# A hybrid decoder layer on one core: adaLN steps behind tile statistics, threshold passes and rotation spread anew, bias rows loaded ahead, low parts of down weights behind the sum of M7, one store from ScalarE

## Chip, cores and metric

One core of a Trainium2 chip runs the whole layer. The metric is the device time in microseconds (us) of one execution, as the median of the runs. Engines: PE is TensorE (PEld is its weight load), DVE is VectorE, ACT is ScalarE, POOL is GpSimd, and SP is the queue that issues DMAs.

## What is computed

One decoder layer on a sequence of 1024 tokens of width 1024, all in float32:

```python
mod = jnp.dot(jax.nn.silu(c), w_ada) + b_ada
shift1, scale1, gate1, shift2, scale2, gate2 = [m[:, None, :] for m in jnp.split(mod, 6, axis=-1)]
h = _rmsnorm(x, norm1_w) * (1.0 + scale1) + shift1
(qa, ka, va, iq, ik, iw, qr, kr, vr, gr, ga, gb) = jnp.split(jnp.dot(h, w_in), ...)
...  # partial rotation of qa, ka, iq, ik over 16 of 64 channels
att = _dsa_attention(qa, ka, va, iq, ik, iw, topk)      # the 256 best keys of each row
y_a = jnp.dot(att, w_attn_proj)
ret = _retention(rotate(qr), rotate(kr) * 128 ** -0.5, vr)   # 4 heads, chunks of 128 tokens
y_r = jnp.dot(jax.nn.silu(gr) * _head_groupnorm(ret, gn_w), w_ret_proj)
merged = jax.nn.sigmoid(ga) * y_a + jax.nn.sigmoid(gb) * y_r
x = x + gate1 * jnp.dot(merged, w_out)
h2 = _rmsnorm(x, norm2_w) * (1.0 + scale2) + shift2
ffn = jnp.dot(jax.nn.silu(jnp.dot(h2, w_ffn_gate)) * jnp.dot(h2, w_ffn_up), w_ffn_down)
out = _rmsnorm(x + gate2 * ffn, final_norm_w)
```

## The kernel before

Nearly every product of two matrices is made of three: each factor is split into a high part, rounded on ACT, and a low part, the difference to it, taken on DVE or POOL; PE multiplies high by high, high by low and low by high. The large projections (the flow of `w_in` after retention, the FFN, the down projection) use a Strassen scheme with seven products, M1 to M7, for a block of two by two.

The order in which each engine works is fixed when the kernel is built. A planner walks through the program and places every instruction on its engine's queue by priority and by estimated times. `turns_after(a, b)` adds an order to that: `a` stands behind `b` on their engine's queue, without a semaphore. An engine works through its queue in order, so an instruction that must wait holds all that stand behind it.

The stages that the change touches, in order of time:

- **Scores and adaLN, from about 130 us.** PE projects V (L121 to L124) and makes index scores (L424, L425); DVE sums the scores (L432). Between them runs `mod_work`, a generator with one step for each of the chunks m = 2, 5, 3, 4 of the adaLN matrix and each k of 8: load 512 KB (`mw`, L515) and add it, scaled, to `macc` on DVE (L525, L527, 1024 columns a step). After the eight steps of m = 2 and m = 5 follows `mod_gate`: for each half it loads a bias row (`gateb`, one buffer, L558), sums `macc` over partitions with a product with `ones` (L561) into a bank of the `lg` tag (three buffers, which the scores use too), adds both on DVE (L562) and stores the result (L563). After m = 3 and m = 4 follows `mod_cols` (transposes and L548 to L552). Every step stands behind the last entry of `summed`, which holds the sums of scores. Sixteen calls fall into the V projection, two into each tile of the loop over `t` with `hp == 0` below, and what is left follows at its end.
- **The threshold passes.** DVE seeks the 256th largest score of each row by 32 counting passes over all scores (L463, six instructions a pass, then L468 and L483), and then makes the mask. `passes[n]` is the first instruction of pass n; some passes are told to stand behind other work by `turns_after`.
- **Retention, two head pairs `hp`.** The projection of q and k is rotated on POOL (L654 to L660). In the loop over nine `t`, `inner(t, e)` makes PE's product of q and k and multiplies it with the decay mask on DVE (L676), `chunk(t - 1, e)` multiplies it with v on PE, carries the state on DVE (L693, L695) and takes the statistics of the tile on DVE (`bn_stats` L701 and `bn_aggr` L702, the last one kept in `chunked[0]`). In the loop's tiles t = 2, 4, 6, 8, `passes[7]` to `passes[10]` (first pair) and `passes[18]` to `passes[21]` (second pair) are put behind that statistic.
- **The flow of 13 streams**, from about 500 us: each stream is 7 products of 12 matmuls (L841, L843, L845). Factors are prepared three products ahead: a sum on DVE (L799, L809), the high part on ACT (L755), the low part on POOL (L756; on DVE near both ends). `add` is the sum of a product into its quarter on DVE (L824). `behind(i)` runs after product i and puts one pass behind the newest sum every seven products. For partial rotation, `rope_load` fetches the 16 channels of q and k and the tables, and `rope_store` does four products on POOL (L991, L992, L994, L995), a difference and a sum on DVE (L993, L996), splits both results (ACT L755, POOL L756) and issues eight stores (L1002).
- **FFN and down projection, to the end.** `Stream.product` is used again. PE adds M4 onto the bank into which M7 was summed, so the first matmul of M4 waits until DVE has read the bank for `add("22")` of M7. `down_slot` makes the factors of the down products: a load, the high part on ACT (L1641), the low part on DVE or POOL (L1642). `final_norm` ends a tile: ACT scales the right half (L1691), DVE the left half (L1693), SP stores both (L1692, L1694).

Of the kernel before, what the change touches and what calls it, by code (L numbers as in the profile page):

```python
# [43 lines left out]
def tile_hybrid_layer(ctx: ExitStack, tc: tile.TileContext, x, c, w_ada, b_ada, norm1_w, w_in,  # L44
# [20 lines left out]
    def f32(ap):  # L65
        return ap.bitcast(F32)
# [433 lines left out]

    st_m = ctx.enter_context(ExitStack())
    modp = pool("modp", side="right", stack=st_m)
    ones = modp.tile([P, P], F32, name="ones")
    nc.vector.memset(ones, 1.0)

    def mod_work():

        steps = [(m, k) for m in (2, 5, 3, 4) for k in range(KT)]
        mw = {}

        def load(n):
            if n < len(steps):
                m, k = steps[n]
                mw[n] = modp.tile([P, D], F32, name="mw", bufs=2)
                ins = nc.sync.dma_start(out=mw[n], in_=w_ada[k * P:(k + 1) * P, m * D:(m + 1) * D])  # L515
                turns_after(ins, loaded[0])

        load(0)
        for n, (m, k) in enumerate(steps):
            load(n + 1)  # L520
            sc = silu_c[:, k:k + 1]
            behind = summed[-1] if summed else None
            if k == 0:
                acc = modp.tile([P, D], F32, name="macc", bufs=1)
                ins = nc.vector.tensor_scalar(acc, mw[n], sc, None, op0=ALU.mult)  # L525
            else:
                ins = nc.vector.scalar_tensor_tensor(acc, mw[n], sc, acc, op0=ALU.mult, op1=ALU.add)  # L527
            if behind is not None:
                turns_after(ins, behind)
            yield  # L530
            if k == KT - 1:
                if m in (2, 5):
                    mod_gate(m, m // 5, acc)
                else:
                    mod_cols(m, m - 3, acc)
                yield
# [14 lines left out]
        if i == 1:  # L551
            nc.vector.scalar_tensor_tensor(d, d, 1.0, colT[:, 64:72], op0=ALU.add, op1=ALU.mult)  # L552

    def mod_gate(m, i, acc):
        for hf in range(2):
            cs = slice(hf * H, (hf + 1) * H)
            g = modp.tile([P, H], F32, name="gateb", bufs=1)
            nc.sync.dma_start(out=g, in_=b_ada[m * D + hf * H:m * D + (hf + 1) * H]  # L558
                              .rearrange("(o d) -> o d", o=1).partition_broadcast(P))
            gp = ps_lg()  # L560
            nc.tensor.matmul(gp, lhsT=ones, rhs=acc[:, cs], start=True, stop=True)  # L561
            nc.vector.tensor_add(g, g, gp)  # L562
            nc.sync.dma_start(out=gate_d[i][:, cs], in_=g)  # L563
# [74 lines left out]
    for hp in range(2):  # L638
# [71 lines left out]
        for t in range(NT + 1):  # L710
# [11 lines left out]
            if t and t % 2 == 0:  # L722
                turns_after(passes[(6, 17)[hp] + t // 2], chunked[0])
            if hp == 0:
                for _ in range(2):
                    next(mgen, None)
            elif t == 2:
# [30 lines left out]
    class Stream:  # L758
# [4 lines left out]

        def __init__(self, env, w, c0):
            self.env, self.w, self.c0 = env, w, c0
            self.c, self.ready, self.blocks = {}, {}, {}
            self.early = ()
            self.next = self.t1 = None

# [51 lines left out]
            self.copied = nc.scalar.activation(self.c[c], ps, AF.Copy)  # L821

        def add(self, c, ps):
            self.env.added = nc.vector.tensor_add(self.c[c], self.c[c], ps)  # L824

        def product(self, m, after=None):

# [157 lines left out]
            nc.sync.dma_start(out=tab[a], in_=rope_c[:, a, cs])  # L985
        return r, tab

    def rope_store(hf, r, tab):
        cs = slice(hf * H, (hf + 1) * H)
        t = [f32(x) for x in ring_pair()]  # L990
        nc.gpsimd.tensor_mul(t[0], r[0], tab[0])  # L991
        nc.gpsimd.tensor_mul(t[1], r[1], tab[1])  # L992
        nc.vector.tensor_sub(t[0], t[0], t[1])  # L993
        nc.gpsimd.tensor_mul(r[0], r[0], tab[1])  # L994
        nc.gpsimd.tensor_mul(r[1], r[1], tab[0])  # L995
        nc.vector.tensor_add(r[1], r[1], r[0])  # L996
        for a, src in enumerate((t[0], r[1])):
            parts = ring_pair()
            split_block(src, *parts)
            for w, dst in enumerate((q_d, k_d)):  # L1000
                for i, part in enumerate(parts):
                    nc.sync.dma_start(out=dst[:, 8 * a:8 * a + 8, i, cs], in_=f32(part[64 * w:64 * w + 64]))  # L1002
# [21 lines left out]
    n_mid = len(seq)  # L1024
    seq += [(st, m) for st in flow[-2:] for m in ("M1", "M2")]
    seq += [(st, m) for m in ("M5", "M6", "M7", "M4", "M3") for st in flow[-2:]]
    rope, staged = {}, {}

    def behind(i):
        n, m = 2 + (i - 14) // 7, seq[i][1]  # L1030
        if i in (11, n_mid - 4):
            genv.lo_engine = None if i == 11 else nc.vector
        if i >= 15 and (i - 15) % 7 == 0 and 24 + (i - 15) // 7 < len(passes) - 1:
            turns_after(passes[24 + (i - 15) // 7], genv.added)
        if 14 <= i < n_mid:
            if m == "M1":
                flow[n + 1].open()
                flow[n].next = flow[n + 1]
            if n == 8 and m in ("M1", "M7"):
                rope[len(rope)] = rope_load(len(rope))  # L1040
            if n == 9 and m in ("M5", "M2"):
                rope_store(int(m == "M2"), *rope[int(m == "M2")])
        if i == n_mid:
            flow[-1].open()
        k = i - n_mid - 4
# [586 lines left out]
    def down_slot(src, lo_eng, scale=None, here=False):  # L1632
# [6 lines left out]
        if scale is not None:  # L1639
            nc.gpsimd.tensor_mul(raw, raw, scale)  # L1640
        nc.scalar.activation(slot[:, 0], raw, AF.Copy)  # L1641
        lo_eng.tensor_sub(slot[:, 1], raw, f32(slot[:, 0]))  # L1642
        return slot[:, 0], slot[:, 1]

    def down_factors(m, p):
# [37 lines left out]
    def final_norm(t, n_parts):  # L1683
# [5 lines left out]
        rs = const.tile([P, 16], F32, name="rs3", bufs=4)[:, 0:1]  # L1689
        nc.gpsimd.tensor_tensor(rs, last, half_pow[:, :1], op=ALU.pow)  # L1690
        nc.scalar.activation(xo[1], xo[1], AF.Copy, scale=rs)  # L1691
        nc.sync.dma_start(out=out[t * P:(t + 1) * P, H:], in_=xo[1])  # L1692
        nc.vector.scalar_tensor_tensor(xo[0], x1[t][:, :H], rs, fnorm[0], op0=ALU.mult, op1=ALU.mult)  # L1693
        nc.sync.dma_start(out=out[t * P:(t + 1) * P, :H], in_=xo[0])  # L1694

# [103 lines left out]
```

## Time and profile before

| | |
|---|---|
| median of 3 runs | 1747.34 us (1744.49 to 1750.73) |
| the profiled execution's own time | 1744.53 us |
| its span, first to last instruction | 1742.7 us |
| PE busy | 1685.4 us, 97% of the span |
| DVE busy | 1234.4 us, 71% |
| POOL busy | 856.8 us, 49% |
| ACT busy | 755.3 us, 43% |
| mean granted clock of PE | 0.995 of full speed |

The busy share of PE says how much of the span it had a matmul in hand; matmuls overlap, so the start of one to the start of the next is the better measure of pace. The idle time in front of a PE instruction, and what ended it, says what the rest of the kernel costs PE.

### The profile page before, as it was taken

What the parts mean: (1) busy time and instruction counts of PE and PEld (TensorE: products, weight loads), DVE (VectorE), ACT (ScalarE), POOL (GpSimd) and SP (SyncE); (2) the same over time, 40 slices, a digit from 0 to 9 for tenths busy, and PEclk for the clock granted to TensorE, in tenths of its full rate; (3) what the DMA queues carried; (4) which work ended last, traced back from release to release, by engine and by line L of the source; (5) the groups of instructions that cost most, each with busy time, mean ns of one, the idle gap of its engine ahead of it and who ended that gap; (6) DMA issues with size and microseconds to landing.
All of it is one profiled execution on the core that took longest, in us unless ns stands there. A gap on an engine that the chain in (4) does not pass through costs nothing.

```text
span 1742.7 us, 24594 instructions
## 1 busy us (share of the span) xinstructions
PE 1685.4 (97%) x8266; PEld 1391.7 (80%) x8266; DVE 1234.4 (71%) x2118; ACT 755.3 (43%) x1469; POOL 856.8 (49%) x855
## 2 busy tenths in 40 slices
PE   5899999999999999999999999999999999999998
PEld 4797777888887887888777888888888888878887
DVE  7528798898899577666576666885666555778664
ACT  3625542332454344530477235643333333445444
POOL 4563274583615578130346550055455554657573
PEclk9999999999999999999999999999999999999999
DMA  9535515412434356865761740044445444586652
GB/s 293 151 95 176 152 55 173 143 34 60 117 98 127 108 151 200 252 205 165 186 142 53 274 169 1 25 133 148 157 134 180 173 146 144 187 305 205 197 169 97
DMA packets 180063, 260.72 MB, mean 150 GB/s; under 512 B 13584, under 2 KB 111328, under 8 KB 177632
## 3 DMA queue, kind: packets, MB, share of 16 engines
q1 hardware_dynamic: 179936, 259.14, 47.6%
q8 instruction: 65, 1.06, 0.3%
q14 instruction: 62, 0.51, 0.1%
HBM read 192.51 MB, written 66.58 MB: 149 GB/s over the span
## 4 chain that ended last, share of the span: by engine, by line
PE 64%; DVE 3%; issue 1%; DMA 1%; POOL 1%; ACT 1%; SPq 0%; POOLq 0%; DVEq 0%; ACTq 0%
PE ya L843 4%; PE ya L841 4%; PE ya L845 4%; PE yb L843 3%; PE yb L841 3%; PE yb L845 3%; PE ya L1664 2%; PE ya L1663 2%; PE ya L1662 2%; PE pva L1183 2%; PE mm L841 2%; PE mm L843 2%; PE mm L845 2%; PE tra L1162 2%; PE lg L841 1%; PE lg L843 1%
## 5 line engine op out<-in xcount | busy, mean ns | idle before, releaser
L80 POOL TENSOR_TENSOR wlo<-wraw,whi 128x512 fp32r<-128x512 f32 (+2 forms) x116 | 147.9, 1285 | 136.6 <-ACT whi L77 100.1
L463 DVE TENSOR_SCALAR_CACHE_REDUCE eq<-score,cand 128x384 uint8<-128x384 f32 (+2 forms) x192 | 180.7, 941 | 4.0
L756 POOL TENSOR_TENSOR flo<-tmp,fhi 128x512 fp32r<-128x512 f32 x79 | 108.2, 1369 | 140.1 <-ACT fhi L755 100.5
L121 PE MATMUL mm<-whi,hT_hi 128*128 128x512 f32 (+1 forms) x432 | 162.0, 380 | 4.0 <-ACT qk L647 1.8
L123 PE MATMUL mm<-wlo,hT_hi 128*128 128x512 f32 (+1 forms) x432 | 161.6, 377 | 0.0
L124 PE MATMUL mm<-whi,hT_lo 128*128 128x512 f32 (+1 forms) x432 | 161.5, 376 | 0.0
L841 PE MATMUL ya<-hc,fhi 128*128 128x512 f32 x344 | 133.9, 390 | 2.0 <-DVE c L824 2.0
L843 PE MATMUL ya<-hc,fhi 128*128 128x512 f32 x344 | 134.1, 390 | 0.6 <-DVE hc L1302 0.6
L845 PE MATMUL ya<-hc,flo 128*128 128x512 f32 x344 | 133.1, 390 | 0.0
L1641 ACT ACTIVATE dslot<-draw 128x512 fp32r<-128x512 f32 x143 | 84.9, 627 | 93.1 <-DMA draw<-act_d 23.2
L756 POOL TENSOR_TENSOR flo<-raws,fhi 128x512 fp32r<-128x512 f32 x60 | 86.3, 1445 | 73.8 <-ACT fhi L755 42.4
L1642 DVE TENSOR_TENSOR dslot<-draw,dslot 128x512 fp32r<-128x512 f32 x81 | 86.4, 1098 | 50.7 <-ACT dslot L1641 49.3
L1642 POOL TENSOR_TENSOR dslot<-draw,dslot 128x512 fp32r<-128x512 f32 x62 | 95.5, 1554 | 53.0 <-ACT dslot L1641 51.0
L77 ACT ACTIVATE whi<-wraw 128x512 fp32r<-128x512 f32 (+2 forms) x116 | 67.2, 591 | 117.3 <-DMA wraw<-in_w_in_dram 56.6
L755 ACT ACTIVATE fhi<-tmp 128x512 fp32r<-128x512 f32 x82 | 51.5, 629 | 111.5 <-PE ya L843 57.2
L843 PE MATMUL yb<-hc,fhi 128*128 128x512 f32 x256 | 99.7, 390 | 0.0
L841 PE MATMUL yb<-hc,fhi 128*128 128x512 f32 x256 | 99.7, 389 | 0.0
L845 PE MATMUL yb<-hc,flo 128*128 128x512 f32 x256 | 99.5, 389 | 0.0
L121 PEld LDWEIGHTS mm<-whi,hT_hi 128*128 128x128 f32 x432 | 81.5, 190 | 16.1 <-ACT qk L647 2.2
L809 DVE TENSOR_TENSOR tmp<-raws 128x512 f32<-128x512 f32 x40 | 30.6, 768 | 86.7 <-POOL flo L756 86.7
L124 PEld LDWEIGHTS mm<-whi,hT_lo 128*128 128x128 f32 x432 | 81.7, 189 | 12.4
L1151 POOL TENSOR_SCALAR sx<-sx,mx 128x128 f32<-128x128 f32 (+7 forms) x64 | 47.4, 747 | 88.9 <-DVE mx L1150 66.3
(419 smaller groups left out, 4959.6 us busy)
## 6 DMA issues: line engine op xcount, KB each, us to landing
draw<-act_d SPq DMA_DIRECT2D x70, 256.0 KB
mw<-in_w_ada_dram SPq DMA_DIRECT2D x32, 512.0 KB
act_d<-c SPq DMA_DIRECT2D x58, 256.0 KB
raw<-in_w_in_dram SPq DMA_DIRECT2D x26, 512.0 KB
raws<-in_w_ffn_gate_dram SPq DMA_DIRECT2D x24, 512.0 KB
raws<-in_w_ffn_up_dram SPq DMA_DIRECT2D x24, 512.0 KB
dw<-in_w_ffn_down_dram SPq DMA_DIRECT2D x22, 512.0 KB
dw_d<-dw SPq DMA_DIRECT2D x10, 1024.0 KB
```

Of the source, the lines that this page charges most:

```text
L77: ins = nc.scalar.activation(hi[:, :n], raw[:, :n], AF.Copy)
L80: nc.gpsimd.tensor_sub(lo[:, :n], raw[:, :n], f32(hi[:, :n]))
L121: ins = nc.tensor.matmul(ps, lhsT=ahi, rhs=whi[:, :n], start=(i == 0), stop=False)
L123: nc.tensor.matmul(ps, lhsT=ahi, rhs=wlo[:, :n], start=False, stop=False)
L124: nc.tensor.matmul(ps, lhsT=alo, rhs=whi[:, :n], start=False, stop=(i == last))
L463: ins = [nc.vector.tensor_scalar(eq[:, :sc.shape[1]], sc, thr[j], None, op0=op, op1=ALU.add, accum_out=cnt[:, j:j + 1]) for j, sc in enume ...
L756: return ins, (eng or nc.gpsimd).tensor_sub(lo, src, f32(hi))
L841: mm = nc.tensor.matmul(ps, lhsT=whi[:, k, :], rhs=hhi[:, k, :], start=own and k == 0, stop=False, skip_group_check=True)
L843: nc.tensor.matmul(ps, lhsT=whi[:, k, :], rhs=hlo[:, k, :], start=False, stop=False, skip_group_check=True)
L845: nc.tensor.matmul(ps, lhsT=wlo[:, k, :], rhs=hhi[:, k, :], start=False, stop=k == 3, skip_group_check=True)
L1641: nc.scalar.activation(slot[:, 0], raw, AF.Copy)
L1642: lo_eng.tensor_sub(slot[:, 1], raw, f32(slot[:, 0]))
```

## The change

- In the loop over tiles of the first head pair, `summed` gets the statistic of the tile before (`chunked[0]`) from t = 1 on, so the adaLN steps issued there stand behind it on DVE.
- The bias row of a gate is loaded whole (512 KB with its copies on 128 partitions) after step k = 3 of its chunk, into one tile of 1024 columns, and both halves are taken from it. `ones` moves into the tile `spare`, which is free at that time.
- In the flow, the passes that stand behind the newest sum every seven products are 22 to 32 instead of 24 to 32.
- `rope_store` becomes the generator `rope_turn` in three turns: the four POOL products; the two DVE instructions; the splits and stores. It is called once a product, M1, M5, M6 for the first half and M3, M7, M2 for the second, where all of it was done at M5 and at M2 before. The second half's loads move from M7 to M6 of the stream before.
- `down_slot` puts the low parts of its calls 2 to 11 that are on DVE (five of them) behind `add("22")` of the last stream.
- The right half of the last tile is stored from ScalarE's queue.

```diff
-    ones = modp.tile([P, P], F32, name="ones")
+    ones = spare[:, :P]
     nc.vector.memset(ones, 1.0)
...
             if behind is not None:
                 turns_after(ins, behind)
+            if k == 3 and m in (2, 5):
+                bias = gate_bias(m)
             yield
             if k == KT - 1:
                 if m in (2, 5):
-                    mod_gate(m, m // 5, acc)
+                    mod_gate(m // 5, acc, bias)
...
+    def gate_bias(m):
+        bias = modp.tile([P, D], F32, name="gateb", bufs=1)
+        nc.sync.dma_start(out=bias, in_=b_ada[m * D:(m + 1) * D].rearrange("(o d) -> o d", o=1).partition_broadcast(P))
+        return bias
+
+    def mod_gate(i, acc, bias):
         for hf in range(2):
             cs = slice(hf * H, (hf + 1) * H)
-            g = modp.tile([P, H], F32, name="gateb", bufs=1)
-            nc.sync.dma_start(out=g, in_=b_ada[m * D + hf * H:m * D + (hf + 1) * H]
-                              .rearrange("(o d) -> o d", o=1).partition_broadcast(P))
+            g = bias[:, cs]
             gp = ps_lg()
             nc.tensor.matmul(gp, lhsT=ones, rhs=acc[:, cs], start=True, stop=True)
             nc.vector.tensor_add(g, g, gp)
...
             if hp == 0:
+                if t:
+                    summed.append(chunked[0])
                 for _ in range(2):
                     next(mgen, None)
...
-            self.env.added = nc.vector.tensor_add(self.c[c], self.c[c], ps)
+            self.env.added = self.added[c] = nc.vector.tensor_add(self.c[c], self.c[c], ps)
...
-    def rope_store(hf, r, tab):
+    def rope_turn(hf, r, tab):
+
         cs = slice(hf * H, (hf + 1) * H)
         t = [f32(x) for x in ring_pair()]
         nc.gpsimd.tensor_mul(t[0], r[0], tab[0])
         nc.gpsimd.tensor_mul(t[1], r[1], tab[1])
-        nc.vector.tensor_sub(t[0], t[0], t[1])
         nc.gpsimd.tensor_mul(r[0], r[0], tab[1])
         nc.gpsimd.tensor_mul(r[1], r[1], tab[0])
+        yield
+        nc.vector.tensor_sub(t[0], t[0], t[1])
         nc.vector.tensor_add(r[1], r[1], r[0])
+        yield
         for a, src in enumerate((t[0], r[1])):
...
-        if i >= 15 and (i - 15) % 7 == 0 and 24 + (i - 15) // 7 < len(passes) - 1:
-            turns_after(passes[24 + (i - 15) // 7], genv.added)
+        if i >= 15 and (i - 15) % 7 == 0 and 22 + (i - 15) // 7 < len(passes) - 1:
+            turns_after(passes[22 + (i - 15) // 7], genv.added)
...
-            if n == 8 and m in ("M1", "M7"):
-                rope[len(rope)] = rope_load(len(rope))
-            if n == 9 and m in ("M5", "M2"):
-                rope_store(int(m == "M2"), *rope[int(m == "M2")])
+            if n == 8 and m in ("M1", "M6"):
+                rope.append(rope_turn(len(rope), *rope_load(len(rope))))
+            if n == 9 and m != "M4":
+                next(rope[int(m in ("M3", "M7", "M2"))], None)
...
-        lo_eng.tensor_sub(slot[:, 1], raw, f32(slot[:, 0]))
+        ins = lo_eng.tensor_sub(slot[:, 1], raw, f32(slot[:, 0]))
+        if 2 <= n < 12 and lo_eng is nc.vector:
+
+            turns_after(ins, flow[-1].added["22"])
...
-        nc.sync.dma_start(out=out[t * P:(t + 1) * P, H:], in_=xo[1])
+        (nc.scalar if n_parts > 1 else nc.sync).dma_start(out=out[t * P:(t + 1) * P, H:], in_=xo[1])
```

## Rows read from the trace of the kernel before

**Rows 1.** The page: the span, PE, and the group of the counting passes

```profile
span 1742.7 us, 24594 instructions
...
PE 1685.4 (97%) x8266; PEld 1391.7 (80%) x8266; DVE 1234.4 (71%) x2118; ACT 755.3 (43%) x1469; POOL 856.8 (49%) x855
...
L463 DVE TENSOR_SCALAR_CACHE_REDUCE eq<-score,cand 128x384 uint8<-128x384 f32 (+2 forms) x192 | 180.7, 941 | 4.0
```

**Rows 2.** Waits of PE: who waited for whom, total us, times, longest us

```profile
PE tr L674 <- DVE inn L676: 4.7, 2, 3.4
...
PE lg L841 <- ACT whi L755: 2.1, 1, 2.1
...
PE mm L841 <- DVE kept L824: 2.0, 1, 2.0
...
PE lg L841 <- ACT kept L821: 1.4, 1, 1.4
```

**Rows 3.** Timeline, 182 to 187 us: start us, us, instruction, [idle before <- releaser]

```profile
182.00 0.33 SPq L558 DMA_DIRECT2D gateb<-in_b_ada_dram  x1
...
185.27 0.69 DVE L562 TENSOR_TENSOR gateb<-gateb,lg 128x512 f32<-128x512 f32 x1 [3.40 <-DMA gateb<-in_b_ada_dram]
...
186.01 0.39 PE L424 MATMUL lg<-khi,qst 128*128 128x256 f32 x1 [1.82 <-DVE gateb L562]
```

**Rows 4.** Timeline, 289 to 291 us, DVE and PE

```profile
289.31 1.28 DVE L527 SCALAR_TENSOR_TENSOR macc<-mw,colT,macc 128x1024 f32<-128x1024 f32 x1 [0.52 <-DMA mw<-in_w_ada_dram]
290.51 0.28 DVE L676 TENSOR_TENSOR inn<-tr,rmask 128x128 f32<-128x128 f32 x1
...
290.85 0.80 PE L674 MATMUL tr<-qkT 128*128 128x128 f32 x2 [3.38 <-DVE inn L676]
```

**Rows 5.** Windows: us, each engine's busy time (instructions), granted clock, DMA share, GB/s

```profile
290.85:294.30 3.45, 3.45 (x10) 2.85 (x10) 3.19 (x4) 0.38 (x1) 0.00 (x0) 0.53 0.58 172
310.00:320.00 10.00, 10.00 (x50) 8.52 (x49) 6.30 (x20) 3.46 (x7) 3.01 (x9) 1.00 0.08 26
340.00:350.00 10.00, 9.97 (x45) 7.97 (x44) 9.52 (x22) 4.39 (x11) 9.05 (x13) 1.00 0.79 251
680.00:690.00 10.00, 10.00 (x45) 8.23 (x44) 6.88 (x9) 2.50 (x4) 10.00 (x8) 1.00 0.66 193
720.00:730.00 10.00, 10.00 (x52) 8.26 (x51) 5.27 (x9) 5.48 (x10) 0.00 (x0) 1.00 0.90 284
```

**Rows 6.** Timeline at 413 us: PE at the first tile of the second pair

```profile
413.51 0.71 PE L674 MATMUL tr<-qkT 128*128 128x128 f32 x4 [1.31 <-DVE inn L676]
```

**Rows 7.** Timeline, 535 to 537 us, DVE and PE

```profile
535.27 0.61 DVE L463 TENSOR_SCALAR_CACHE_REDUCE eq<-score,cand 128x384 uint8<-128x384 f32 x1
...
536.54 0.50 PE L841 MATMUL mm<-hT_hi,whi 128*128 128x512 f32 x1 [2.01 <-DVE kept L824]
```

**Rows 8.** Timeline, 668 to 675 us, around the first rotation

```profile
668.00 1.74 POOL L995 TENSOR_TENSOR wlo<-wlo,whi 128x512 f32<-128x512 f32 x1
...
673.61 0.63 ACT L755 ACTIVATE whi<-whi 128x512 fp32r<-128x512 f32 x1 [2.78 <-DVE whi L993]
674.32 1.29 POOL L756 TENSOR_TENSOR wlo<-whi 128x512 fp32r<-128x512 f32 x1 [4.57 <-ACT whi L755]
```

**Rows 9.** Timeline, 1525 to 1530 us, DVE and PE

```profile
1525.01 1.77 DVE L1642 TENSOR_TENSOR dslot<-draw,dslot 128x512 fp32r<-128x512 f32 x1
...
1527.31 0.68 DVE L1642 TENSOR_TENSOR dslot<-draw,dslot 128x512 fp32r<-128x512 f32 x1
...
1528.52 0.68 DVE L824 TENSOR_TENSOR c<-c,ya 128x512 f32<-128x512 f32 x1
...
1529.25 0.50 PE L841 MATMUL ya<-hc,fhi 128*128 128x512 f32 x1 [1.68 <-DVE c L824]
```

**Rows 10.** Timeline at the end: the two last stores

```profile
1738.54 0.33 SPq L1692 DMA_DIRECT2D out_dram<-xo  x1
1739.28 0.33 SPq L1694 DMA_DIRECT2D out_dram<-xo  x1
```

More of the change, by code (lines that the diff above doesn't have):

```diff
@@ L552, in mod_cols @@
             nc.vector.scalar_tensor_tensor(d, d, 1.0, colT[:, 64:72], op0=ALU.add, op1=ALU.mult)
-    def mod_gate(m, i, acc):
+    def gate_bias(m):
[3 more added lines that the diff above has]
+    def mod_gate(i, acc, bias):
         for hf in range(2):
             cs = slice(hf * H, (hf + 1) * H)
-            g = modp.tile([P, H], F32, name="gateb", bufs=1)
-            nc.sync.dma_start(out=g, in_=b_ada[m * D + hf * H:m * D + (hf + 1) * H]
-                              .rearrange("(o d) -> o d", o=1).partition_broadcast(P))
+            g = bias[:, cs]
             gp = ps_lg()
@@ L765, in __init__ @@
             self.env, self.w, self.c0 = env, w, c0
-            self.c, self.ready, self.blocks = {}, {}, {}
+            self.c, self.ready, self.blocks, self.added = {}, {}, {}, {}
             self.early = ()
@@ L1026, in tile_hybrid_layer @@
     seq += [(st, m) for m in ("M5", "M6", "M7", "M4", "M3") for st in flow[-2:]]
-    rope, staged = {}, {}
+    rope, staged = [], {}
     def behind(i):
```

## Prediction

> **What bounds the kernel now.** The page comes first: PE is busy 1685.4 of 1742.7 us, 97% [rows 1]. No other engine comes near it, so the kernel can only gain where PE stands idle or runs at the low clock, 57 us in all, part of it at the start, which the change doesn't touch. The second view is the list of what PE waited for, the third the timeline around each of those waits. After the start only a few waits exceed 1 us, and the parts of the change lie beside five of these places: at 184 us for a bias row [rows 3], at 287 us for the mask product of a retention tile [rows 4], at 534 us for a sum [rows 7], between 670 and 695 us around the rotation [rows 2, 8] and at 1527 us for the sum of M7 [rows 9]. In each of them an engine's queue, worked in order, held the awaited instruction behind something else. So each part is read by one question: what stands in front of the awaited instruction afterwards.
>
> **Bias rows.** One buffer for two halves: SP issues the load of the second half only at 182.00, when the first half's store has landed; DVE stands 3.40 us for it, and PE 1.82 us, since the second product's bank is one of the three that the scores use [rows 3]. The change loads the whole row four steps earlier, with the same bytes, and both halves are added at once. What hides the load are the four steps between; on SP it stands in front of later `mw` loads only, and if that cover were gone the old wait would stay. PE gets back 1.8 (0 to 1.8). DVE gets its 3.4 too, but it has no other work there on which PE waits. `ones` in `spare` costs nothing: its first new writer comes hundreds of us later.
>
> **adaLN steps.** At 287 us PE stands 3.38 us for L676 [rows 4]. In front of it DVE has steps of m = 3, 1.28 us each, and one of them stands another 0.52 for its load. After that wait ten matmuls run at a granted clock of 0.53 for 3.45 us [rows 5], the lower of the two levels (1.2 instead of 2.4 GHz): 3.45 x 0.47 = 1.6 us lost. With the change no step of m = 3 can stand in front of the first tile's statistic, so both losses, 5.0 in all, lose their cause. What is late next is shown by the second head pair, where no adaLN step exists: its first tile still waits 1.31 us for L676, behind a counting pass [rows 6], and keeps its clock. I let that wait appear in the first pair too: 3.4 + 1.6 - 1.3 = 3.7 (0 to 5.0).
> The steps don't vanish. Eight of m = 3 and seven of m = 4 now follow statistics in the tile loop: 15 x 1.28 = 19.2 us of DVE, where eight of m = 4 ran there before. DVE is busy 6.30 of 10 us at 310 us, so 3.7 are free there, and 9.52 at 340 us with steps in it, while PE stays at 9.97 [rows 5]: that is the cover. Their loads wait for the buffer that a step frees; behind them in SP's queue stand stores of retention tiles (four buffers) and weight loads for the next pair. If a step is late, these are late too; I take 0, and 1.3, the wait of rows 6, if that cover fails. The last steps push the passes behind the eighth tile by some 4 us, which the free time above can take again.
>
> **Passes.** A pass is 180.7 / 32 = 5.6 us of counting [rows 1]. At 535 us DVE starts the next pass in front of the sum for which PE stands 2.01 us [rows 7]. With 22 and 23 held back, two passes, some 11 us, leave the DVE queue before the flow's third stream, so this sum is no longer late: 2.0 (0 to 2.0). Two passes now run among the last streams, where DVE is busy 5.27 of 10 us [rows 5]. That cover is wide; without it, make_g waits for up to one counting instruction at a time, about 1 us. The mask is made after `made` as before, so attention isn't held.
>
> **Rotation.** Two waits, 1.4 and 2.1 [rows 2]. The timeline shows a knot: POOL's four products end at 668.00 + 1.74, then ACT stands 2.78 us for L993, and POOL 4.57 us for ACT, with the factors of the next products behind both [rows 8]. In three turns, one product (12 matmuls) apart, ACT and DVE no longer stand for what was just begun, and the second half starts two products earlier. But POOL has the same work, and it is busy 10.00 of 10 us at 680 [rows 5], where the second wait grows. I take the first wait in full and half of the second, 2.4, up to 3.5. Below nothing: where a POOL product and a two-input DVE instruction meet, it takes 1.74 instead of 1.29, as the rows 8 show; if four more do so, POOL is 4 x 0.45 = 1.8 us later: -1.8.
> The Trainium skill, "SBUF — State Buffer", section "Who interferes with whom", says that a DVE instruction with two SBUF inputs and a GpSimd instruction that reads SBUF share a port pair, and that the second blocks fully until the first is done. It speaks against the gain of spreading: by it each moved product could stand for a whole DVE instruction. The rows agree that such instructions get longer, by 0.45 and not by a whole one.
>
> **Low parts behind M7.** Before the sum of M7 (L824 at 1528.52) DVE does L1642, 1.77 us beside POOL and 0.68 without it; PE stands 1.68 us [rows 9]. Five L1642 move behind that sum. The down products that need their low parts come after 12 matmuls of M4 or of the first slot, so there is time. What is late next is DVE's other work, but the five took more than PE's wait: 1.7 (0 to 1.7).
>
> **Store.** The stores issue at 1738.54 and 1739.28 [rows 10]. From ScalarE the first no longer stands in front of the second: at most 0.7. But the bytes of both still go out, and a first DMA on ScalarE's queue isn't in the trace, so -0.3 (an issue of 0.33) to 0.7; I take 0.2, near to nothing, as the store itself is no shorter.
> The Trainium skill, "DMA: Bandwidth & Descriptors", section "Issuing engines are not separate DMA queues", says that such a split saves only the time to issue; by it the term would be 0.3, and no row here shows a second queue.
>
> **Sum.** 1.8 + 3.7 + 2.0 + 2.4 + 1.7 + 0.2 = 11.8. On the profiled execution (1744.5: its span of 1742.7 and 1.8 around it) that gives 1732.7. The median of the runs, 1747.3, lies 2.8 above it; I forecast the median, 1747.3 - 11.8 = 1735.5. With all upper ends (1.8 + 5.0 + 2.0 + 3.5 + 1.7 + 0.7 = 14.7) the profiled execution would be at 1729.8.
>
> **Rivals.**
> - *The rotation does not pay.* POOL is full at 680 us [rows 5], so its lateness returns as the same waits plus 1.8: 11.8 - 2.4 - 1.8 = 7.6, 1739.7. Against it: POOL stood idle 4.57 us in the knot itself [rows 8].
> - *The late work comes back.* DVE and POOL do as much as before, and the planner places every instruction anew. Then only what has no successor stays: 1.8 for the bias, 1.6 of clock, 1.7 at M7, 5.1 in all: 1742.2. For it: the wait of rows 6 has no adaLN step in front of it.
> - *It does nothing.* The new orders hold already in the planner's result, or waits of the same size open beside them: 1746 to 1747. Against it: rows 3, 4 and 9 show the opposite order.
> - *Slower: steps in front of the tiles.* In the first pair's loop each step stands behind one tile's statistic, but may stand in front of the next tile's L676 or L695, as L527 did in rows 4. Fifteen steps passed on to PE in full cost 19.2; without the adaLN term the rest gives 8.1, so 1747.3 + 11.1 = 1758.4. It turns the sign from the seventh step on (7 x 1.28 = 9.0). Against it: at 340 us the steps of m = 4 stand among the tiles and PE waits for nothing [rows 5].
>
> **How the numbers follow.** Forecast 0.47 (its own range 1729 to 1740), rotation 0.17, late work 0.20, nothing 0.06, slower 0.10. From 1729, the upper ends, to 1745, which takes in the first two rivals and the runs' scatter, lie about 0.8. About 0.3% (5.2 us) is what a measurement of this kernel can tell from no change, so faster means below 1742.1: the forecast, the rotation rival and half of the late work, less a little for scatter, 0.72; same 0.18; slower 0.10.
>
> **What would show it.** Right: no L562 waiting for a DMA and no PE wait on it; no L527 in front of the first L676 and no half clock there; L824 directly behind M7's matmuls; ACT without a wait for L993 over 1 us. Wrong: PE waits on L676, L695 or `mm` of the second pair in 300 to 420 us, waits on `ms` or gT_lo at 705 to 780, or POOL still full up to 700 with PE waiting for L755. If PE's idle time between 100 us and the end falls by less than 5 us, the sum was wrong, and the list of PE's waits tells which term.

## The result: 1735.3 us, and the profile after

The changed kernel takes 1735.34 us in the median (1731.86 to 1740.23), the kernel before 1747.79 beside it; the ratio is 0.9925, 95% interval 0.9899 to 0.9951. That is 12.4 us, and the forecast median was 1735.5. The two profiled executions are much closer: a span of 1738.1 us here, 1742.7 before [rows 1]. So 4.7 of the 12.4 us lie in the traces of one execution of each, and the rest in how the executions scatter: the profiled execution of before (1744.49) is the shortest of its six, that of the changed kernel (1739.87) the second longest of its six. Both parts have to be explained.

The page of the changed kernel, its span, its engines and the counting passes. PE works as long as before, so what was gained is idle time of PE or low clock. Below the page are two windows, of before and of the changed kernel, from 100 us to the end (length, PE's busy time and its matmuls, then the other engines): PE's idle time there falls from 29.1 to 25.6 us.

```profile
span 1738.1 us, 24581 instructions
...
PE 1686.4 (97%) x8266; PEld 1392.7 (80%) x8266; DVE 1235.6 (71%) x2118; ACT 753.4 (43%) x1469; POOL 863.2 (50%) x855
...
L463 DVE TENSOR_SCALAR_CACHE_REDUCE eq<-score,cand 128x384 uint8<-128x384 f32 (+2 forms) x192 | 180.8, 941 | 3.9
```

```profile
100.00:1742.70 1642.70, 1613.56 (x7884) 1331.17 (x7883) 1174.03 (x2002) 706.65 (x1385) 809.23 (x784) 1.00 0.47 146
100.00:1738.10 1638.10, 1612.54 (x7895) 1330.88 (x7893) 1175.66 (x2002) 704.88 (x1385) 815.99 (x785) 1.00 0.47 146
```

What PE waits for in the changed kernel (who for whom, total us, times, longest), beside [rows 2]. L674, L676, L841, L824, L821 and L755 of before are now L679, L681, L848, L831, L828 and L762.

```profile
PE tr L668 <- POOL rq L665: 4.4, 1, 4.4
...
PE lg L134 <- ACT whi L77: 3.1, 1, 3.1
...
PE mm L848 <- ACT kept L828: 1.5, 1, 1.5
PE ya L848 <- DVE c L831: 1.4, 2, 1.0
...
PE mm L850 <- DVE hT_lo L641: 1.1, 1, 1.1
...
PE tr L679 <- DVE inn L681: 0.3, 1, 0.3
```

Of the 4.7 us for the mask product 0.3 are left, and the 1.8 us for the gate row are gone. In their place stands a wait of 4.4 us for a rotated query, which before did not have, and ahead of both one of 3.1 us at 57 us, where before waits 1.2 us. The timeline of the changed kernel from 266 to 286 us shows its chain (start, duration, instruction, idle time before it and its releaser), and the window behind it the clock.

```profile
266.88 1.30 POOL L80 TENSOR_TENSOR wlo<-wraw,whi 128x512 fp32r<-128x512 f32 x1
266.95 7.22 DVE L468 TENSOR_SCALAR rej<-cnt 128x6 int32<-128x6 f32 x1
...
275.85 0.69 DVE L567 TENSOR_TENSOR gateb<-gateb,lg 128x512 f32<-128x512 f32 x1
276.56 0.33 SPq L568 DMA_DIRECT2D gate_d<-gateb  x1
...
279.77 0.63 ACT L77 ACTIVATE whi<-wraw 128x512 fp32r<-128x512 f32 x1 [10.04 <-DMA wraw<-in_w_in_dram]
280.48 1.27 POOL L80 TENSOR_TENSOR wlo<-wraw,whi 128x512 fp32r<-128x512 f32 x1 [6.34 <-ACT whi L77]
...
283.89 0.45 POOL L664 TENSOR_TENSOR rq<-rra,rrb 128x128 f32<-128x128 f32 x1
...
285.23 0.48 PE L668 MATMUL tr<-ident,rq 128*128 128x128 f32 x1 [4.39 <-POOL rq L665]
```

```profile
285.23:288.70 3.47, 3.47 (x12) 3.00 (x13) 3.15 (x9) 0.60 (x1) 0.35 (x1) 0.51 0.21 65
```

It begins with a tiny instruction: L468, six numbers per partition at the end of a counting pass. Alone it takes 0.17 us (the row at 389 us, at the end of the experiments); here it lasts 7.22, as long as POOL works its row of products without a pause. Behind it in DVE's queue stands the sum of the second gate row (L567); SP's next instruction is that row's store (L568); the weight loads of the next head pair stand behind the store; ScalarE waits 10.04 us for one of them, POOL 6.34 us for ScalarE, and the rotation of the last tile stands behind POOL's L80. PE waits 4.39 us and then runs 3.47 us at a granted clock of 0.51, the lower of the two levels: 4.4 + 3.47 x 0.49 = 6.1 us.

The other places, in the changed kernel: the first tile of the second pair [rows 6], the flow's first long wait (now for the low parts of hT, not for the sum of [rows 7]), the rotation [rows 8] (L1004 is its difference, L993 of before, and L1005 its sum), M7's sum [rows 9] and the two last stores [rows 10].

```profile
415.38 0.71 PE L679 MATMUL tr<-qkT 128*128 128x128 f32 x4 [0.33 <-DVE inn L681]
...
521.84 0.50 PE L850 MATMUL mm<-hT_lo,whi 128*128 128x512 f32 x1 [1.10 <-DVE hT_lo L641]
...
666.85 0.63 ACT L762 ACTIVATE whi<-whi 128x512 fp32r<-128x512 f32 x1 [1.75 <-DVE whi L1004]
...
668.51 0.50 PE L848 MATMUL mm<-S,whi 128*128 128x512 f32 x1 [1.51 <-ACT kept L828]
...
671.75 0.63 ACT L762 ACTIVATE whi<-wlo 128x512 fp32r<-128x512 f32 x1 [2.80 <-DVE wlo L1005]
...
1518.88 1.77 DVE L1475 TENSOR_TENSOR c<-c,c 128x512 f32<-128x512 f32 x1
...
1520.58 0.67 DVE L831 TENSOR_TENSOR c<-c,ya 128x512 f32<-128x512 f32 x1
...
1521.30 0.50 PE L848 MATMUL ya<-hc,fhi 128*128 128x512 f32 x1 [1.04 <-DVE c L831]
...
1733.75 0.40 ACTq L1705 DMA_DIRECT2D out_dram<-xo  x1
1733.78 0.33 SPq L1707 DMA_DIRECT2D out_dram<-xo  x1
```

### The profile page after: what moved, and what is told of

The parts are those of the page before. It is cut to its first block, busy times and chain, and to the rows that moved or that the text cites. A ratio compares the mean times of both kernels' runs of the same rounds, so it can differ in the third digit from the quotient of the medians.

```text
span 1738.1 us, 24581 instructions
## 1 busy us (share of the span) xinstructions
PE 1686.4 (97%) x8266; PEld 1392.7 (80%) x8266; DVE 1235.6 (71%) x2118; ACT 753.4 (43%) x1469; POOL 863.2 (50%) x855
## 4 chain that ended last, share of the span: by engine, by line
PE 61%; DVE 4%; DMA 3%; issue 1%; ACT 1%; SPq 1%; POOL 0%; POOLq 0%; DVEq 0%; ACTq 0%
PE ya L850 4%; PE ya L848 4%; PE ya L852 4%; PE yb L848 3%; PE yb L852 3%; PE yb L850 3%; PE ya L1677 3%; PE ya L1675 3%; PE pva L1193 3%; PE ya L1676 3%; PE tra L1172 2%; PE mm L850 2%; PE mm L848 2%; PE mm L852 2%; PE ya L124 1%; PE ya L121 1%
## 5 line engine op out<-in xcount | busy, mean ns | idle before, releaser
L80 POOL TENSOR_TENSOR wlo<-wraw,whi 128x512 fp32r<-128x512 f32 (+2 forms) x116 | 146.9, 1278 | 140.6 <-ACT whi L77 98.0
L848 PE MATMUL ya<-hc,fhi 128*128 128x512 f32 x344 | 133.8, 390 | 1.4 <-DVE c L831 1.4
L77 ACT ACTIVATE whi<-wraw 128x512 fp32r<-128x512 f32 (+2 forms) x116 | 66.8, 590 | 124.8 <-DMA wraw<-in_w_in_dram 61.9
L762 ACT ACTIVATE fhi<-tmp 128x512 fp32r<-128x512 f32 x82 | 51.5, 629 | 111.5 <-PE ya L850 57.2
L848 PE MATMUL yb<-hc,fhi 128*128 128x512 f32 x256 | 99.6, 389 | 0.0
```

Source lines behind the costliest of these rows:

```text
L77: ins = nc.scalar.activation(hi[:, :n], raw[:, :n], AF.Copy)
L80: nc.gpsimd.tensor_sub(lo[:, :n], raw[:, :n], f32(hi[:, :n]))
L848: mm = nc.tensor.matmul(ps, lhsT=whi[:, k, :], rhs=hhi[:, k, :], start=own and k == 0, stop=False, skip_group_check=True)
```

## Experiments

Each edit below is described by where it first moves an instruction in an engine's order. That matters: an edit in the flow leaves everything ahead of 500 us in place, and some edits move nothing but what they name. The runs e1 to e4 were on one chip, e5 to e11 on a second and e12 on a third, so medians are compared across them with care; each ratio is to before in the same sitting.

**The changed kernel again (e1)**, and with a small edit that turned out to leave the order of every engine as it was (e3); so both are the changed kernel's order.

```
-            nc.sync.dma_start(out=gate_d[i][:, cs], in_=g)
+            ins = nc.sync.dma_start(out=gate_d[i][:, cs], in_=g)
+            if i == 1:
+                turns_after(ins, last_load[0])        # e3: the last load so far stood ahead anyway
```

> The changed kernel as it is, for a second profile beside the first, whose span of 1738.1 us holds a new wait of 4.39 us of PE for the rotation of a query (280.4 to 285.2 us, then 3.5 us of low clock), behind a tiny DVE instruction that lasted 7.22 us while POOL worked. Theory (it belongs to the order of the instructions): the wait is there again, 3 to 5 us, and the span is near 1735 to 1738. Rival (an accident of one execution): no wait over 2 us there, and a span of 1730 to 1733. The median is 1732 to 1739 by both.

> The changed kernel, with the two stores of the second gate row ordered behind the weight loads of the first head pair on SP's queue; nothing else. Theory (the store held the weight loads, these held ScalarE and POOL, and so the rotation and PE): ScalarE has no wait near 10 us for a weight load at 280 us, PE's wait for the rotated query falls from 4.4 us to under 1 and the half clock behind it goes: 4 to 6 us less than the changed kernel, 1729 to 1732. Rival (the rotation is late because DVE and POOL stand in each other's way): the wait stays over 3 us, 1734 to 1737. By the prediction's sum the term of the adaLN steps is then paid in full, 1731.6.

e1: 1735.92 us (ratio 0.993, 0.9906 to 0.9955), profiled span 1737.5, PE's wait for L665 4.32 us. e3: 1736.23 us (0.9941, 0.9916 to 0.9966), span 1735.2, wait 4.40 us. The chain belongs to the order, not to one execution (e9 below shows that the order alone doesn't force it). Neither theory of e3 was tested by it, since the loads that stand behind the store are those of the next pair, made later.

**Without the adaLN line (e2, and once more as e7).**

```
                 if hp == 0:
-                    if t:
-                        summed.append(chunked[0])
```

> The changed kernel without the line that places the adaLN steps behind tile statistics. By the prediction's term it is 3.7 us slower, 1739. By the reading of the two traces (5.0 us of wait and low clock for L676 gone, 4.4 + 1.6 us of a new wait for the rotation of a query come) it is equal within 1.5 us, 1734 to 1737, with a wait of 2 to 4 us for the mask product back at the first retention tile and none over 2 us for the rotation. Rival (every edit re-plans everything, terms mean little): a change of over 3 us in either direction with waits at places that none of the terms names.

> The changed kernel without the adaLN line once more, for the profile of an execution that may be one of its long ones (1750 to 1754; the profile of e2 was at 1744.5). Theory: in a long one the first retention tile waits longer, behind adaLN steps whose loads come later, with more of the low clock, 6 to 9 us more between 280 and 330 us and elsewhere the same. Rival: the lost time lies elsewhere (start, attention) or evenly over the span.

e2: 1750.55 us (1740.75 to 1754.23; ratio 1.0003, 0.998 to 1.0026): 14.6 us slower than e1, where the prediction had 3.7 and the reading of the traces none; so the rival's number came. Its wait for the rotated query is 3.44 us, where under 2 was expected: that wait doesn't come from the adaLN line. Its profiled execution is a short one (span 1742.7) and shows only 5.1 of that. The first waits of its tiles, and a counting pass in between:

```profile
294.21 1.28 DVE L527 SCALAR_TENSOR_TENSOR macc<-mw,colT,macc 128x1024 f32<-128x1024 f32 x1 [0.71 <-DMA mw<-in_w_ada_dram]
...
296.55 0.80 PE L679 MATMUL tr<-qkT 128*128 128x128 f32 x2 [4.64 <-DVE inn L681]
...
398.94 0.70 DVE L468 TENSOR_SCALAR rej<-cnt 128x6 int32<-128x6 f32 x1
...
419.14 0.49 PE L679 MATMUL tr<-qkT 128*128 128x128 f32 x2 [1.11 <-DVE inn L681]
```

e7 is the same program in a long execution: 1754.77 us, span 1753.0. Theory said that its surplus lies at the first pair's first tile. It does not: that wait is 2.90 us, and up to 410 us e7 is 2.3 us ahead of e2. At the last mask product it is 6.5 us behind (462.07 against 455.53). In between lies the second pair's first tile, behind the same tiny instruction of the same pass:

```profile
396.61 8.78 DVE L468 TENSOR_SCALAR rej<-cnt 128x6 int32<-128x6 f32 x1
...
404.88 0.48 POOL L665 TENSOR_TENSOR kk<-rra,rrb 128x128 f32<-128x128 f32 x1
405.43 0.17 DVE L483 SCALAR_TENSOR_TENSOR cand<-cand,rej 128x6 int32<-128x6 int32 x1
...
423.15 0.79 PE L679 MATMUL tr<-qkT 128*128 128x128 f32 x2 [7.44 <-DVE inn L681]
```

0.70 us in e2, 8.78 us here, until POOL's row ends at 405.36. The wait is 6.3 us longer, and low clock follows; a further 2 us come in the flow (2.62 us for L826 instead of 1.51, with low clock behind it). So one program's times differ by 10 us, most of it through when a tiny instruction meets POOL's row.

**The line alone, on the kernel before (e5), and the kernel before again (e8).** e5 adds the two lines of e2 to the kernel before; its orders are those of before up to 274 us.

> The kernel before plus one line: the adaLN steps in the tile loop go behind the tiles' statistics. Up to 270 us its order on every engine is that of before. By the prediction's term it gains 3.7 us, 1742.5 against a median of 1746 to 1747 of before. Theory from the run without the line (1750.6, the changed kernel 1735.9 beside it): the line removes more than one execution of before showed, since the times of both kernels without it scatter over 14 us, up to 1754, and those with it over 7: 1738 to 1741, no time over 1745, and no long wait of PE for L676 at the first tile. Rival (the line only undoes a harm that the other parts do together): within 3 us of before, with times up to 1754.

> The kernel before once more, for a second profile beside the first (1744.5); its other times reach from 1740 to 1755. Theory: if this execution is a long one, its surplus lies between 280 and 330 us, at the first retention tiles; if it is a short one, the waits are as in the first profile within 1 us. Rival: the surplus lies elsewhere.

e5: 1742.73 us against 1745.55 of before (ratio 0.998, 0.9962 to 0.9997), 2.8 us: the prediction's 3.7 and the rival's "within 3" fit it, and with an interval of 0.5 to 6.6 us the theory's 5 to 8 isn't excluded; its bounds on single times (none over 1745) are, by 1750.6. Its profiled execution holds no wait at the first pair's first tile, but one at the second's: the hold is 6.42 us there.

```profile
PE tr L674 <- DVE inn L676: 4.6, 1, 4.6
...
PE mm L845 <- DVE hT_lo L636: 2.9, 2, 2.1
PE lg L843 <- ACT whi L757: 2.2, 1, 2.2
...
PE ya L843 <- DVE c L826: 2.0, 2, 1.6
```

It also shows the other parts undone: 2.9 us for low parts where the changed kernel waits 1.1, 2.2 us in the rotation, 1.6 at M7, and 1.9 for the gate row. And it has no wait for a rotated query: its L468 at 269 us lasts 1.19. e8 was a short execution, 1745.95 us, with the waits of the first profile behind 100 us within 0.3 us but three: 0.8 instead of 1.8 us for the gate row, 0.2 instead of 1.4 for L821 and 0.1 instead of 0.7 for a load in attention. The first two differ by more than the 1 us that was expected, so a wait of one profile is not yet its size.

**The gate row's stores later (e6).** Only SP's order changes: the stores go behind the first tile's statistic, so the next pair's loads go ahead.

```
-            nc.sync.dma_start(out=gate_d[i][:, cs], in_=g)
+            stored.append((gate_d[i][:, cs], g))       # issued at a later step, for m = 5 two steps
+                                                       # into m = 3, with turns_after(ins, chunked[0])
```

> The changed kernel with the stores of each gate row issued later: the second row's behind the first tile's statistic, so that the weight loads of the next head pair stand in front of it on SP's queue. Only SP's order changes. The edit of e3 had the same aim but left every engine's order as it was. Theory (store holds loads, loads hold ScalarE and POOL, POOL holds the rotation of the query): ScalarE's wait of 10 us and PE's of 4.4 go, with the half clock behind it: 1729 to 1732. Rival (DVE is held 7.2 us by POOL's row of products and the rotation is late anyway): 1734 to 1737 and a wait over 3 us for the rotation.

1739.78 us against 1745.55 (0.9962, 0.9948 to 0.9977): by the medians it is some 4 us slower than the changed kernel (on another chip), slower than both ranges expected. The first half of the theory holds: ScalarE waits no more than 1.33 us for a load at 266 to 273 us and PE's wait for L665 is gone. But the loads feed POOL, whose row now has no pause, and it holds L468 for 11.39 us; the mask product is behind it.

```profile
266.96 11.39 DVE L468 TENSOR_SCALAR rej<-cnt 128x6 int32<-128x6 f32 x1
...
292.55 0.79 PE L686 MATMUL tr<-qkT 128*128 128x128 f32 x2 [6.67 <-DVE inn L688]
```

**The tiny instruction in its other form (e9, e10, e11).** The orders stay, but for six tiny instructions on POOL that fill a table of powers of two and a few matmuls of the first 130 us that trade places.

```
-            nc.vector.tensor_scalar(rej, cnt, float(TOPK), float(value), op0=ALU.is_lt, op1=ALU.mult)
+            nc.vector.scalar_tensor_tensor(rej, cnt, float(TOPK), pw[:, bit:bit + 1].to_broadcast([P, n]),
+                                           op0=ALU.is_lt, op1=ALU.mult)
```

> The changed kernel with one tiny instruction of each counting pass in another form: the rejection (six values per partition) as scalar_tensor_tensor with the power of two from a small table, not as tensor_scalar. The order of the instructions on every engine stays, but for six tiny ones on POOL that fill the table. In the traces so far the tensor_scalar form is held for up to 11.4 us while POOL works its products back to back, and the two-input form (L483) for 1.3 at most. Theory (this instruction, held by POOL, holds DVE, then the gate row's sum, its stores, the weight loads and the rotation): none of them over 1.5 us, PE's wait of 4.4 us at 280 us and the low clock behind it go: 1729 to 1732. Rival (POOL or the loads are late anyway): 1734 to 1737 with PE's wait still over 3 us.

> The kernel before with the same other form of the tiny instruction, orders as in before. Theory (the long times of before, 1750 to 1755, are executions in which that instruction is held for 6 to 9 us in front of the second head pair's first tile): they go, all times within 1738 to 1746, median 1741 to 1743 against 1746 of before. Rival (long times come from the adaLN loads in front of the first pair's first tile): median 1744 to 1748, with times over 1750.

> The changed kernel without the adaLN line, with the same other form of the tiny instruction. Theory: the 1750.6 of e2 falls by 8 to 12 us, to 1739 to 1743, with no time over 1746, and against e9 it shows what the line is worth by itself: by the prediction's term 3.7 us, by the waits in e2 and e7 for L679 and the low clock behind them 5 to 8. Rival (the line was worth 14.6 us by what it does to the adaLN steps alone): still about 14 us above e9, times up to 1754.

e9 (the changed kernel): 1734.88 us (1729.61 to 1736.56; ratio 0.9917, 0.9895 to 0.9939), not to be told from the changed kernel. e10 (before): 1744.48 (0.9981, 0.9963 to 0.9999). e11 (without the line): 1742.38 (0.9977, 0.9959 to 0.9994), where e2 had 1750.55 on another chip. The form is not the cause of the hold: the two-input form is held as well, and the expectation that it stays under 1.5 us fell. Whether it makes holds rarer stays open: e11's median came where the theory had it, but with times of 1749 and 1751 (one of 12 over 1750, six of 12 in e2); e9 and e10 came within their rivals' medians, e10 with two times over 1750. In e9's profile POOL lets it in at the end of the running product, in e11's, begun as early in the same product, only when the row ends. First e9, then e11:

```profile
265.69 1.27 POOL L80 TENSOR_TENSOR wlo<-wraw,whi 128x512 fp32r<-128x512 f32 x1
265.76 1.22 DVE L472 SCALAR_TENSOR_TENSOR rej<-cnt,rank 128x6 int32<-128x6 f32 x1
266.91 0.47 POOL L670 TENSOR_TENSOR rq<-rra,rrb 128x128 f32<-128x128 f32 x1
```

```profile
266.14 1.31 POOL L80 TENSOR_TENSOR wlo<-wraw,whi 128x512 fp32r<-128x512 f32 x1
266.23 7.21 DVE L472 SCALAR_TENSOR_TENSOR rej<-cnt,rank 128x6 int32<-128x6 f32 x1
...
272.67 0.74 POOL L666 TENSOR_TENSOR rrb<-qk,sinr 128x256 f32<-128x256 f32 x1
273.47 0.17 DVE L488 SCALAR_TENSOR_TENSOR cand<-cand,rej 128x6 int32<-128x6 int32 x1
```

What e9's profile is worth is the counter-test of the chain: with the hold at 1.22 us, the wait for the rotated query, the low clock behind it and every wait over 0.5 us for a mask product are gone. The span is 1727.8 us, 9.7 less than e1's: 2.4 of it ahead of 230 us, 4.6 between 230 and the first chunk (286.3 against 293.3), 1.6 up to 475 us, 1.2 behind. Between 260 us and that chunk it gains 6.2 us, the size of the chain; a stretch of low clock at 232 us, which e1 lacks, costs it 1.6 before that. Such an execution is one of several: its other times reach to 1736.6.

**The old rotation (e4)**: turns at M5 and M2, load at M7, the difference behind the first two products and the sum behind all four.

> The changed kernel with the rotation as before: both sums behind the first two products, load at M7, one turn each at M5 and M2. By the prediction's term 2.4 us slower, 1737.7; by the waits of PE between 660 and 705 us in the two traces (3.7 before, 2.1 after) 1.6 slower, 1737. Rival (POOL is full, the spread pays nothing): 1734 to 1736, with PE's waits there between 1.8 and 2.5 us as now.

1738.21 us (0.9954, 0.9935 to 0.9973), 2.3 more than e1 on the same chip; eleven of its twelve times lie above seven of e1's eight. PE waits 2.07 us there, and a stretch of low clock follows (window: length, PE, ..., granted clock 0.54, 1.6 us lost):

```profile
688.13 0.63 PE L848 MATMUL lg<-hT_hi,whi 128*128 128x512 f32 x1 [2.07 <-ACT whi L762]
...
688.10:691.50 3.40, 3.37 (x8) 2.61 (x9) 3.40 (x5) 2.05 (x5) 3.40 (x4) 0.54 0.52 183
```

The profiles show less than the medians: from the flow's first product to its last e4 takes 256.3 us, the changed kernel 255.7, 255.4 (e1) and 254.9 (e3), so 0.6 to 1.4 us.

**Old passes and low parts (e12)**: 24 for 22, and no order behind M7's sum. Up to 510 us every order is the changed kernel's.

> The changed kernel with two parts undone: counting passes held back from the 24th on, as before, and the low parts of the down weights not behind M7's sum. By the prediction's terms 2.0 + 1.7 = 3.7 us slower, 1739. By the waits that the traces show at these two places (e5 beside the changed kernel: 2.06 + 0.83 against 1.10 us at 520 to 530, 1.64 against 1.04 at the sum of M7) 2.4 us, 1737.5 to 1738. Rival (waits of the same size open beside them, neither pays): 1734 to 1736.

1737.40 us (0.9937, 0.9915 to 0.9960), which lies between the prediction's 3.7 and none and can't tell them apart. Its trace does: 2.6 us of PE's waits between 528 and 557 us in four pieces (1.23, 0.41, 0.62, 0.31), and 1.67 us at M7's sum. By chance the profiled execution is its longest (1747.39), and shows that the changed kernel's own order has the long hold too. The same instruction in e12, and then in the changed kernel's profile:

```profile
389.03 10.74 DVE L468 TENSOR_SCALAR rej<-cnt 128x6 int32<-128x6 f32 x1
...
399.23 0.51 POOL L665 TENSOR_TENSOR kk<-rra,rrb 128x128 f32<-128x128 f32 x1
...
399.82 1.31 POOL L659 TENSOR_TENSOR rra<-qk,cosr 128x512 f32<-128x512 f32 x1
...
421.63 1.22 PE L679 MATMUL tr<-qkT 128*128 128x128 f32 x4 [6.68 <-DVE inn L681]
```

```profile
389.12 0.17 DVE L468 TENSOR_SCALAR rej<-cnt 128x6 int32<-128x6 f32 x1
```

The hold in e12 ends at 399.77, between a POOL product that ends at 399.74 and one that begins at 399.82: a pause of 0.08 us was enough. Five more holds, of 3.4 to 4.6 us near 400 us (the changed kernel, e1, e3, e4, e6), end in the same pause.

## Why the prediction was right, and where its steps were not

The median came out as forecast, and the sign for the reason given: waits went in which an in-order queue held an awaited instruction behind something else. But the sum of 11.8 was not paid term by term, and by the prediction's own sign it was wrong: PE's idle time from 100 us to the end fell by 3.6 us, less than the 5 it named. That the median fell by 12.4 all the same is luck as far as the sum goes: the sum was read from one short execution of before, and long executions became rarer, which no term named.

- **Bias rows, 1.8**: the wait of rows 3 is gone in every trace of the changed order. The four traces with the old loads show 1.8, 0.8, 1.9 (e5) and 0.4 us, so 1.8 is near the upper end. Right as a wait. But "on SP it stands in front of later `mw` loads only" missed the other end: the hold of 7.2 us at 267 us appears (ten traces with the bias part: nine of 7.2 to 11.4 us and e9's 1.2; four without it: 0.4 to 1.2 us). e2, e4 and e12 each take out other parts and keep the hold, and the last store acts at the end only, so this new wait, 6.1 us, came with the bias part; that is by elimination, as no run takes out the bias part alone. It came with another cost: the prediction had the start as a place "which the change doesn't touch" and `ones` in `spare` as free, but the orders differ from about 30 us on. In all ten traces PE waits 3.1 us for L77 at 57 us (1.2 to 1.9 in the four others), and the first score product of the changed kernel begins 1.6 us later (137.9 against 136.4).
- **adaLN steps, 3.7**: both losses at the first tile are gone, as forecast, and the wait let appear at the second pair is 0.3 instead of 1.3. Short executions with and without the line differ by 5.1 us (e2, e1), the upper end. Alone on the kernel before it is worth 2.8 in the median (e5), beside the other parts 14.6 (e2), 7.5 with the other form (e11 against e9). What makes it more than its waits is how often an execution is a long one. Of the times of before 23 of 87 are 1750 us or more, of e2 6 of 12, of the changed order (the runs of the result, e1, e3) none of 22. Where the surplus sits is shown for e7 and e12; that it sits there in the long times of before too is by analogy, since both of its profiles are short ones. Why the line makes them rarer isn't shown, and e5, with the line, has a hold of 6.42 us there too.
- **Passes, 2.0**: the wait of rows 7 is gone, but the low parts of hT wait 1.1 us where they waited 0.3: 1.2 paid. e12 shows 2.6 at this stage against 1.1, so 1.5.
- **Rotation, 2.4**: the waits went from 3.7 us [rows 2, with 0.2 for a third] to 2.1, so 1.6, but not as forecast. The first wait, taken in full, is still there: 1.51 us at 668.51, since ScalarE waits 1.75 us for the difference L1004, which stands behind counting instructions on DVE, and makes `kept` right behind. So the sign named for "right", ScalarE without a wait over 1 us for L993 (now L1004), did not come. The second wait, taken by half, is gone. The two errors cancel in part. In e5, e8 and e10, which have the old rotation, the first wait is only 0.2 us; beside them the spread trades a wait of 2.2 us, and the low clock that follows it in e4 and e8 alone, for one of 1.5. The median of e4 (2.3) has the term's size; where it comes from is shown only for 0.6 to 1.4 us.
- **Low parts behind M7, 1.7**: 0.6 was paid (1.67 in e12, 1.04 in the changed kernel). L831 does not stand directly behind M7's matmuls, as the sign had it: the last of them ends at 1517.09, and DVE then does L1533 and L1475, 1.77 us beside POOL where L1465, the same instruction, took 0.68 in before; the sum begins as L1475 ends. The step that failed is "What is late next is DVE's other work, but the five took more than PE's wait". e9 has the same order there, but an L1533 ahead of these, beside POOL for 1.70 us in the changed kernel, takes 0.69, DVE is a microsecond earlier, and PE's idle time is 0.02 us: the rest can be had.
- **Store, 0.2**: nothing. Both stores now issue within 0.03 us, as the prediction allowed, but the end lies 7.3 us behind PE's last product, 7.2 before.
- **The sum**: terms paid in the changed kernel's profile: 1.8 + 5.0 + 1.0 (the second pair's first tile, 1.3 to 0.3) + 1.2 + 1.6 + 0.6 = 11.2, and 6.1 back at the rotated query: 5.1 against the 4.7 of the spans (one stretch of low clock at 233 us that only before shows, 1.7, and the 1.6 us ahead of the first scores nearly cancel). With the hold at 267 us short in both, the profiles of e10 and e9 differ by 1739.0 - 1727.8 = 11.2; that this is the same number is chance: in e9 all of M7's wait is gone too, and it has the low clock at 232 us. The median has the rest from rarer long executions.

The step that failed most is the paragraph on shared access: "The rows agree that such instructions get longer, by 0.45 and not by a whole one". They agreed in rows 8, for POOL. Rows 9 already had DVE's side: L1642 takes 1.77 us beside POOL and 0.68 without it, 1.1 longer. The Trainium skill, "SBUF — State Buffer", section "Who interferes with whom", has the second of two instructions that contend block until the first is done; the runs show more, a hold over a whole row of POOL instructions, ten in e7. The rival "the late work comes back" (1742.2) was near in kind, but named neither place nor cause: a wait took the place of the removed one, not because DVE had as much work but because it stood still. The slower rival did not come: at 340 to 350 us DVE is busy 9.95 of 10 us with steps in it and PE 10.00.

Open: what lets DVE in at the end of one POOL product and not at the next, in the same order; and whether a pause put into POOL's row would save time: the pauses of 0.08 us in the traces do end a hold, but placing one was not tried. No version here is shown to beat the changed kernel; e9's median is 1 us lower, within the intervals.

## What to carry to other kernels

Before a term is taken as paid, follow what the freed engine does next, up to the next engine with which it shares an access: a short instruction at the end of a pass can hold a whole queue, and SP's stores carry that to loads of another stage. Where the times of one program scatter by more than the term, take a second profile and a long execution; here one trace of each explained 4.7 us of 12.4. When PE waits for a sum, look at what its engine did before it, not only at what PE did. And feeding an engine earlier (e6) is no gain if its pauses were what another engine lived on.

## What the runs showed of the hardware

- A DVE instruction on 128x6 numbers, 0.17 us alone, lasts 7.2, 8.8, 10.7 or 11.4 us (and others from 2.1 to 6.4) beside a row of POOL products with all operands in SBUF, and ends with POOL's first pause, within 0.1 us, even where that pause is 0.08 us; this holds for `tensor_scalar` and for `scalar_tensor_tensor` with two inputs in SBUF. In other cases it gets in at the end of the running product (1.2 us).
- The counting instructions (`tensor_scalar` with its accumulated output) beside the same rows keep their length: 192 of them, none over 1.29 us; the largest form takes 1.28 us in the mean, beside POOL's products and without them. The same section of the Trainium skill leaves this form out of those that contend, and the traces agree.
- A DVE instruction with two 128x512 inputs in SBUF takes 0.68 us alone and 1.77 beside POOL's products (L1465 in before, L1475 in the changed kernel).
- A wait of PE of 4.4 us was followed by 3.5 us at a granted clock of 0.51 (0.52 in e1). Behind 100 us, in the 14 traces, every wait of 2.6 us or more was followed by a stretch at the lower level, those of 1.8 to 2.2 us in 8 of 25 cases (2.07 in e4 was, 2.12 in before wasn't), and none of 1.0 to 1.7 us was.
